# The modulation's 1024-column loads and their bias rows issued by GpSimd instead of SyncE

## The chip, the cores and the metric

The kernel runs on one core of one Trainium2 chip. Five engines work side by side, each on its own instructions in its own fixed order, and wait for one another through semaphores: TensorE (PE) multiplies matrices, VectorE (DVE) and ScalarE (ACT) work on elements, GpSimd (POOL) does small odds and ends, and SyncE (SP) does nothing but issue DMA transfers. The metric is the time of one execution on the device in microseconds (us). A matmul of this kernel mostly multiplies a 128x128 stationary block with 128x512 moving columns.

## What is computed

Two decoder layers over 256 tokens of width 2048. In each layer a conditioning vector is turned into six vectors of length 2048, the modulation, and these shift, scale and gate two sub-layers:

```python
c_act = jax.nn.silu(c)
for l in range(DEPTH):
    mod = c_act @ w_mod[l] + b_mod[l]
    shift1, scale1, gate1, shift2, scale2, gate2 = jnp.split(mod[:, None, :], 6, axis=-1)
    h = rms_norm(x, norm1_gain[l]) * (1.0 + scale1) + shift1
    x = x + gate1 * hybrid_token_mixer(h, ..., w_in[l], ..., w_out[l])
    h = rms_norm(x, norm2_gain[l]) * (1.0 + scale2) + shift2
    x = x + gate2 * swiglu_ffn(h, ffn_w_gate[l], ffn_w_up[l], ffn_w_down[l])
return rms_norm(x, final_norm_gain)
```

The token mixer projects `h` with `w_in`, runs three mixers on parts of the columns (gated linear attention, sliding-window attention, gated delta rule) and projects back with `w_out`. The feed-forward part (FFN) has 5632 hidden columns. All arrays are float32.

## The kernel before

**Weights.** Every projection goes through `stream`: for each block of 128 input rows k (a *job*) SyncE loads 128x1024 weights, 512 KB, into one of three buffers `raw` (L323). ACT rounds them to `wh` (L330), DVE takes the rest `wl = raw - wh` (L331), and PE multiplies with both parts for two blocks of tokens (L358): 12 matmuls for a job. `wh` and `wl` have three buffers each. In some projections the weights are used whole, without L330 and L331.

**Modulation.** `mod @ w_mod` is one vector times a matrix, so it isn't done on PE. `mod_segment` cuts it into segments of 1024 columns with 16 steps each (512 columns for the first two vectors of layer 0, called early). A step loads 512 KB of `w_mod` into one of **two** buffers `mraw` (L220), and DVE multiplies by a column of `c_act` and adds to the accumulator `acc` (L223, a SCALAR_TENSOR_TENSOR, STT below). The first step of a segment clears `acc` on POOL (L212) and loads the bias into its first row (L213). `acc` has two buffers. `finish` sums over the partitions on PE. For the vectors of later use there are 20 such segments with 320 steps; the early ones use buffers `g` and 128 loads of 256 KB.

**What sets the order.** In the program the steps are called from `tick`, so many for each job (`RATE_...`). A scheduler then orders each engine's instructions by the program's priority and by when each could start, and so takes a step ahead of its place in the program where its engine is free and its buffers are. What is on one engine stays in this order on the chip: an instruction whose semaphore is late holds up all that stands behind it. Before the change SyncE issues 1341 rows, with the loads of weights and of the modulation in one row; POOL has 122 rows, among them the small powers for the norms (`rms`, `grs`, `qkrs`, L408), values for the attention's sinks (L891) and the memsets.

## Time and profile before

| | |
|---|---|
| median of 3 runs | 2582.44 us (2582.32 to 2587.12) |
| the profiled execution | 2585.34 us, of which the span 2583.5 us |
| mean granted TensorE clock | 0.986 |
| busy share of the span | PE 94%, DVE 66%, ACT 41%, POOL 2% |
| DMA | 600.79 MB, mean 233 GB/s |
| loads of `w_mod` in steps of 1024 columns | 320 of 512 KB, issued by SPq |
| their work on DVE (L223) | 320 of 1282 ns |

Busy is the time in which an engine had an instruction running; queue and semaphore instructions don't count. SPq is SyncE issuing DMAs. The granted clock is at nine tenths or more in all but one of the profile's 40 slices. A matmul counts as busy while it waits in the pipeline as well, so that how many jobs pass in a stretch says more about PE than its busy share does.

### The profile page before, as it was taken

The page shows a single profiled execution, that of the slowest core. Times are in us where ns is not written, and L with a number is a line of the kernel's source. Part 1 is how long each engine was busy: PE and PEld are TensorE (multiplying, and loading weights), DVE is VectorE, ACT ScalarE, POOL GpSimd, SP SyncE. Part 2 cuts the span into 40 slices and gives each one's busy share as a digit, 9 for nine tenths or more (in the row PEclk, how much of TensorE's full clock was granted, in tenths as well). Part 3 has the DMA queues.
Part 4 walks back from the last instruction along what each step waited for, and adds up shares of the span by engine and source line. Part 5 has one row for each costly group of instructions (what it writes and reads, how often), then busy time and mean ns, then how long its engine had stood idle before and what let it go on. Part 6 is the DMA issues. An engine that isn't in the chain of part 4 may idle for free.

```text
span 2583.5 us, 30803 instructions
## 1 busy us (share of the span) xinstructions
PE 2432.7 (94%) x11164; PEld 1884.1 (73%) x11164; DVE 1714.4 (66%) x2171; ACT 1053.5 (41%) x1548; POOL 58.2 (2%) x117
## 2 busy tenths in 40 slices
PE   4999998889999988999999999999999999999998
PEld 2555785447878767788877878877778878888876
DVE  6767867576675777657578785888664575544555
ACT  2203443124444333344335454564644434344443
POOL 1000000000000000000000000000000000000000
PEclk9999999989999999999999999999999999999999
DMA  9996538777778888868687861675676686666654
GB/s 341 368 322 204 180 114 282 258 231 268 261 259 260 283 268 274 292 193 286 223 277 261 281 192 50 214 232 192 212 256 193 200 286 195 188 191 188 189 184 155
DMA packets 190033, 600.79 MB, mean 233 GB/s; under 512 B 21628, under 2 KB 26268, under 8 KB 189496
## 3 DMA queue, kind: packets, MB, share of 16 engines
q1 hardware_dynamic: 189880, 598.81, 70.7%
q8 instruction: 88, 1.44, 0.2%
q14 instruction: 65, 0.53, 0.1%
HBM read 596.63 MB, written 2.10 MB: 232 GB/s over the span
## 4 chain that ended last, share of the span: by engine, by line
PE 57%; DMA 20%; DVE 10%; issue 8%; ACT 4%; POOL 1%; SPq 1%; DVEq 0%; ACTq 0%; POOLq 0%
PE acc L358 48%; DMA mraw<-in_w_mod 13%; DVE wl L331 4%; DMA raw<-in_w_down 3%; DMA raw<-in_w_in 2%; DVE acc L223 2%; ACT wh L330 1%; PE mm L403 1%; PE ga L895 1%; DMA raw<-in_w_up 1%; PE mm L678 1%; PE mm L685 1%; PE ga L916 1%; DMA raw<-in_w_gate 1%; PE fin L248 1%
## 5 line engine op out<-in xcount | busy, mean ns | idle before, releaser
L358 PE MATMUL acc<-wh,hm 128*128 128x512 f32 (+3 forms) x4872 | 1339.2, 389 | 20.9 <-DVE xs L931 4.7
L330 ACT ACTIVATE wh<-raw 128x1024 fp32r<-128x1024 f32 (+3 forms) x669 | 684.7, 1025 | 985.8 <-PE acc L358 548.9
L331 DVE TENSOR_TENSOR wl<-raw,wh 128x1024 fp32r<-128x1024 f32 (+3 forms) x669 | 785.2, 1179 | 446.6 <-ACT wh L330 444.5
L358 PEld LDWEIGHTS acc<-wh,hm 128*128 128x128 f32 x4872 | 892.0, 189 | 215.8 <-issue 25.5
L358 PE MATMUL acc<-wl,hm 128*128 128x512 f32 (+3 forms) x2484 | 792.3, 394 | 12.2 <-DVE wl L331 9.7
L223 DVE SCALAR_TENSOR_TENSOR acc<-mraw,c_act,acc 128x1024 f32<-128x1024 f32 x320 | 410.3, 1282 | 225.2 <-DMA mraw<-in_w_mod 222.9
L358 PEld LDWEIGHTS acc<-wl,hm 128*128 128x128 f32 x2484 | 458.4, 190 | 124.1 <-DVE wl L331 22.3
L358 PE MATMUL acc<-wh,ahl 128*128 128x512 f32 x560 | 158.4, 397 | 0.0
L358 PEld LDWEIGHTS acc<-wh,ahl 128*128 128x128 f32 x560 | 105.8, 189 | 24.5
L358 PE MATMUL acc<-wl,ahl 128*128 128x512 f32 x280 | 90.8, 398 | 7.2 <-DVE wl L331 7.2
L223 DVE SCALAR_TENSOR_TENSOR g<-g,c_act,g 128x512 f32<-128x512 f32 x128 | 88.7, 747 | 12.6 <-DMA g<-in_w_mod 12.4
L358 PE MATMUL acc<-wh,b 128*128 128x512 f32 (+2 forms) x184 | 74.7, 545 | 2.2 <-ACT b L447 2.1
L358 PE MATMUL acc<-wl,b 128*128 128x512 f32 (+2 forms) x176 | 67.1, 518 | 2.6 <-DVE g L969 2.6
L358 PEld LDWEIGHTS acc<-wl,ahl 128*128 128x128 f32 x280 | 52.2, 189 | 23.1 <-DVE wl L331 11.3
L358 PE MATMUL acc<-raw,b 128*128 128x512 f32 (+2 forms) x176 | 67.6, 524 | 0.0
L358 PEld LDWEIGHTS acc<-wh,b 128*128 128x128 f32 x184 | 35.2, 197 | 30.8 <-issue 23.1
L358 PEld LDWEIGHTS acc<-wl,b 128*128 128x128 f32 x176 | 32.8, 192 | 29.2 <-issue 20.3
L416 ACT ACTIVATE acc<-xs 128x512 f32<-128x512 f32 x32 | 19.0, 595 | 85.7 <-DVE xs L931 85.7
L447 ACT ACTIVATE b<-mm,mod,mod 128x128 f32<-128x128 f32 x24 | 9.2, 461 | 109.7 <-DVE mod L256 92.1
L358 PEld LDWEIGHTS acc<-raw,b 128*128 128x128 f32 x176 | 33.5, 195 | 26.7 <-issue 21.7
L929 DVE TENSOR_TENSOR acc<-acc,gate 128x512 f32<-128x512 f32 x64 | 43.0, 695 | 10.3 <-PE acc L358 10.2
L358 PE MATMUL acc<-raw,hm 128*128 128x512 f32 x88 | 41.7, 598 | 1.4 <-ACT acc L416 1.4
(314 smaller groups left out, 1645.8 us busy)
## 6 DMA issues: line engine op xcount, KB each, us to landing
mraw<-in_w_mod SPq DMA_DIRECT2D x320, 512.0 KB
raw<-in_w_down SPq DMA_DIRECT2D x176, 512.0 KB
raw<-in_w_gate SPq DMA_DIRECT2D x160, 512.0 KB
raw<-in_w_up SPq DMA_DIRECT2D x160, 512.0 KB
raw<-in_w_in SPq DMA_DIRECT2D x72, 512.0 KB
g<-in_w_mod SPq DMA_DIRECT2D x128, 256.0 KB
raw<-in_w_out SPq DMA_DIRECT2D x43, 512.0 KB
raw<-in_w_in SPq DMA_DIRECT2D x32, 264.0 KB
```

Of the source, the lines that this page charges most:

```text
L223: V.scalar_tensor_tensor(acc, raw[:, a], c_act[:, i + a:i + a + 1], acc, ALU.mult, ALU.add)
L248: TE.transpose(ps[:, i * P:(i + 1) * P], acc[:, (j + i) * P:(j + i + 1) * P], ident)
L330: A.activation(wh[:, :width], raw[:, :width], AF.Copy)
L331: V.tensor_tensor(wl[:, :width], raw[:, :width], wh[:, :width].bitcast(F32), ALU.subtract)
L358: TE.matmul(ps[blk, j][:, :segs[j][2]], xa, parts[j][part], start=i == 0 and n == 0, stop=last and n == len(terms) - 1)
L403: TE.transpose(ps[:, j * P:(j + 1) * P], src[:, j * P:(j + 1) * P], ident)
L416: A.activation(scr[0]() if junk is None else junk, xs[:, blk, j * 512:(j + 1) * 512], AF.Square, accum_out=ssq[blk][:, j:j + 1])
L678: TE.matmul(ps[:, s], LT[blk][:, s], Tm[blk][:, s], start=True, stop=True)
L685: TE.matmul(ps[:, s], U[blk][:, s], m1[:, s], start=True, stop=True)
L895: TE.matmul(ps[:, j * nk:(j + 1) * nk], qT[rows, i + j], kT[rows, g, :nk], start=True, stop=True)
L916: TE.matmul(ps[:, j * 64:(j + 1) * 64], pT[:, j * nk + kb * P:j * nk + (kb + 1) * P], kv[kb][:, P + g * 64:P + (g + 1) * 64], start=kb == ...
L929: V.tensor_tensor(ps, ps, need(gate_row, (l, part, j)), ALU.mult)
```

## The change

In `mod_segment` the loads of `mraw` and the bias rows that belong to them are issued with `nc.gpsimd` (`G`) and no longer with `nc.sync` (`SY`). The early steps stay with SyncE, and so do the two buffers `mraw`, the data, the sizes and the arithmetic.

```diff
             if i == 0:
                 st["acc"] = scr[1]() if early else tl(accp, [P, 1024], "acc")
                 G.memset(st["acc"][:, :width], 0.0)
-                SY.dma_start(st["acc"][0:1, :width], b_mod[l:l + 1, c0:c0 + width])
+                (SY if early else G).dma_start(st["acc"][0:1, :width], b_mod[l:l + 1, c0:c0 + width])
             acc = st["acc"][:, :width]
             n = min(rows, KD - i)
             raw = scr[1]() if early else tl(modp, [P, 1024], "mraw")
             if hold:
                 G.tensor_copy(raw[:, 0:1], hold.pop())
             raw = raw[:, :n * width].rearrange("p (a n) -> p a n", a=n)
-            SY.dma_start(raw, w_mod[l, i * P:(i + n) * P, c0:c0 + width]
-                         .rearrange("(a p) n -> p a n", p=P))
+            (SY if early else G).dma_start(raw, w_mod[l, i * P:(i + n) * P, c0:c0 + width]
+                                           .rearrange("(a p) n -> p a n", p=P))
```

SyncE's queue loses 340 rows, 320 loads and 20 bias rows, and POOL's gains them (122 to 462). The scheduler orders all engines anew from there. First the beginning of POOL's queue, before the first norm (`ss` is the sum of squares, `rms` its power, `acc_1231` and `acc_2032` the two halves of the first gate vector of layer 0, `g` an early accumulator):

```order
 L212 MEMSET acc_1231 128x1024
+L220 DMA mraw_1234<-in_w_mod 128x1024
+L213 DMA acc_1231<-in_b_mod 1x16x64
+L220 DMA mraw_1243<-in_w_mod 128x1024
 L212 MEMSET acc_2032 128x1024
+L213 DMA acc_2032<-in_b_mod 1x16x64
+L220 DMA mraw_1246<-in_w_mod 128x1024
 L212 MEMSET g_211 128x512
+L220 DMA mraw_1255<-in_w_mod 128x1024
+L220 DMA mraw_1268<-in_w_mod 128x1024
 L408 ISA
 L408 TENSOR_TENSOR rms_38_179<-ss_37_176,half_100 128x1
```

Five loads of the gate vector now stand ahead of the first norm, at the very start. In SyncE's queue before, they stood behind the weights of nearly the whole first projection (the first was issued at 160.93 us). Twenty of them stand in POOL's queue ahead of the memsets for the last block of that projection.

The same place on DVE, just after the angles' sines are prepared (the rows on `g` are early modulation steps, which the first norm needs):

```order
+L223 SCALAR_TENSOR_TENSOR acc_1231<-mraw_1234,c_act_102,acc_1231 128x1024
+L223 SCALAR_TENSOR_TENSOR acc_1231<-mraw_1243,c_act_102,acc_1231 128x1024
+L223 SCALAR_TENSOR_TENSOR acc_1231<-mraw_1246,c_act_102,acc_1231 128x1024
 L421 TENSOR_REDUCE ss_37_176<-ssp_32_167 128x1
+L223 SCALAR_TENSOR_TENSOR g_205<-g_208,c_act_102,g_205 128x512
 L422 TENSOR_SCALAR ss_37_176<-ss_37_176 128x1
-L223 SCALAR_TENSOR_TENSOR g_205<-g_208,c_act_102,g_205 128x512
+L223 SCALAR_TENSOR_TENSOR acc_1231<-mraw_1255,c_act_102,acc_1231 128x1024
```

Three, then four steps of the gate vector stand ahead of the early steps. Eight have come before the first early sum is complete.

Then DVE in the FFN of layer 0, in the second chunk's gate and up projections (`acc_9745` is a segment of the modulation of layer 1). Before:

```order
L223 SCALAR_TENSOR_TENSOR acc_9745<-mraw_9811,c_act_102,acc_9745 128x1024
L331 TENSOR_TENSOR wl_8272<-raw_8269,wh_8271 128x1024
L331 TENSOR_TENSOR wl_8290<-raw_8287,wh_8289 128x1024
L223 SCALAR_TENSOR_TENSOR acc_9745<-mraw_9850,c_act_102,acc_9745 128x1024
L331 TENSOR_TENSOR wl_8308<-raw_8305,wh_8307 128x1024
L331 TENSOR_TENSOR wl_8329<-raw_8326,wh_8328 128x1024
L223 SCALAR_TENSOR_TENSOR acc_9745<-mraw_9871,c_act_102,acc_9745 128x1024
```

and with the change, on the same engine:

```order
L331 TENSOR_TENSOR wl_8272<-raw_8269,wh_8271 128x1024
L223 SCALAR_TENSOR_TENSOR acc_9745<-mraw_9850,c_act_102,acc_9745 128x1024
L331 TENSOR_TENSOR wl_8290<-raw_8287,wh_8289 128x1024
L223 SCALAR_TENSOR_TENSOR acc_9745<-mraw_9871,c_act_102,acc_9745 128x1024
L331 TENSOR_TENSOR wl_8308<-raw_8305,wh_8307 128x1024
L223 SCALAR_TENSOR_TENSOR acc_9745<-mraw_9892,c_act_102,acc_9745 128x1024
```

Where a step stood for about every one and a half jobs, one now stands for nearly every job. So it is in all ten segments of this kind (eight in the FFN of layer 0, two in that of layer 1): their 16 steps stood among 19 to 24 jobs and stand among 14 to 17. After a segment more jobs follow without a step.

## The prediction

> **What bounds the kernel now.** I read the chain of work that ended last first, then the groups by line, then SyncE's own waits.

> ```profile
> PE 57%; DMA 20%; DVE 10%; issue 8%; ACT 4%; POOL 1%; SPq 1%; DVEq 0%; ACTq 0%; POOLq 0%
> L331 DVE TENSOR_TENSOR wl<-raw,wh 128x1024 fp32r<-128x1024 f32 (+3 forms) x669 | 785.2, 1179 | 446.6 <-ACT wh L330 444.5
> L223 DVE SCALAR_TENSOR_TENSOR acc<-mraw,c_act,acc 128x1024 f32<-128x1024 f32 x320 | 410.3, 1282 | 225.2 <-DMA mraw<-in_w_mod 222.9 <-DMA acc<-in_b_mod 0.2
> SPq L323 <- DVE wl L331: 1343.6, 634, 12.5
> SPq L220 <- DVE acc L223: 221.4, 162, 4.4
> ```

> PE carries the kernel, but a fifth of the chain is DMA, and DVE sat idle for 222.9 us until a modulation load had landed. SyncE waited 221.4 us with such a load at its head until a step had freed one of the two buffers; weights queue behind it meanwhile. The change touches both waits.

> To see what these cost PE I count jobs. L331 runs once for a job, so its count in a stretch is the number of jobs. First come the ten segments in which modulation runs beside the FFN (columns: stretch, its length, DVE busy with L331 and its count, clock, DMA share, GB/s), then two stretches of FFN without any.

> ```profile
> 593.00:663.00 70.00, 29.17 (x24) 1.00 0.87 303
> 686.00:745.00 59.00, 22.98 (x19) 1.00 0.87 297
> 800.00:860.00 60.00, 22.94 (x19) 1.00 0.87 301
> 867.00:937.00 70.00, 26.36 (x22) 0.98 0.84 271
> 945.00:1014.00 69.00, 26.47 (x22) 1.00 0.85 280
> 1022.00:1083.00 61.00, 25.44 (x21) 1.00 0.84 283
> 1169.00:1234.00 65.00, 28.35 (x24) 1.00 0.88 297
> 1287.00:1352.00 65.00, 23.03 (x19) 1.00 0.82 278
> 1846.00:1915.00 69.00, 28.25 (x24) 1.00 0.84 290
> 2067.00:2130.00 63.00, 25.19 (x21) 1.00 0.83 286
> ...
> 2150.00:2310.00 160.00, 70.59 (x58) 1.00 0.61 191
> 2310.00:2470.00 160.00, 69.85 (x57) 1.00 0.62 188
> ```

> Without modulation a job takes 320 us / 115 = 2.78 us, which is PE's own pace. The ten segments have 215 jobs in 651 us; at 2.78 us they would take 598. So modulation beside the FFN costs 53 us now, **5.3 us a segment**, and that is all this change could win there.

> What sets the pace of a segment stands in the chain in order of time (start, length, what):

> ```profile
> 818.49 6.18 DMA mraw<-in_w_mod
> ...
> 825.97 1.23 DVE wl L331
> 827.20 0.02 issue
> 827.22 0.33 SPq L323
> 827.55 0.05 issue
> 827.60 6.86 DMA mraw<-in_w_mod
> ...
> 837.38 5.02 DMA mraw<-in_w_mod
> ```

> This is one buffer going round: a load lands, the step runs (1.28 us by its row above), SyncE still has a weights load ahead that waits for an L331 (1.23), issues it (0.33), and only then the next modulation load. From 827.60 to 837.38 is 9.78 us for one buffer, so 4.9 for a step with two; over the whole segment, 16 steps, about 4.0.

> **The change, part by part.**

> *1. The cycle of a buffer in the FFN.* The weights load ahead goes away: 1.23 + 0.33 and the small gaps, 1.6 us. Left are the landing, (6.18 + 6.86 + 5.02) / 3 = 6.0 us, and the step, 1.28. What POOL adds over SyncE (whose 0.33 or so is in the landing) isn't in this trace, since POOL issues no DMA in it. These are the nearest rows:

> ```profile
> L212 POOL MEMSET g<- 128x512 f32 x8 | 4.4, 552 | 89.3 <-DVE g L223 51.9 <-DMA g<-in_consts 36.2 <-issue 0.8
> L408 POOL TENSOR_TENSOR qkrs<-qkss,half 128x16 f32<-128x16 f32 x2 | 5.8, 2920 | 167.7 <-DVE qkss L596 167.7
> L1032 POOL MEMSET b<- 128x1 f32 x4 | 0.3, 99 | 0.0
> ```

> POOL's cheapest instruction takes 0.1 us and its dearest 2.9; these are the bounds. [...] The cycle is then 6.0 + 1.28 + 0.55 = 7.83 us, or **3.9 us a step** (bounds 3.7 and 5.1; a quicker landing in less traffic, the 5.02 of one piece, gives 3.4).

> What is new is the order. A segment now stands among about 16 jobs on DVE, one step to a job, and DVE can't pass a step whose load is late. PE needs 16 x 2.78 = 44.5 us for these jobs, the steps need 15 x 3.9 = 58.5: 14 us lost. PE has three `wl` buffers and so about one job in hand when a segment starts, 2.8 us of cover that refills where no steps are. 14 - 2.8 = 11.2, less the 5.3 lost already, is 5.9 a segment, **+59 us** for ten. At 3.4 us it is -1.6 a segment (-16), at 5.1 us it is 76.5 - 44.5 - 8.1 = +24 (+240).

> [...]

> *2. The head.* Twenty loads come from 160 us and later into the start. These rows (PE, PEld, DVE, ACT, POOL busy with counts, clock, DMA share, GB/s) show what they meet:

> ```profile
> 20.00:40.00 20.00, 2.23 (x8) 1.43 (x8) 18.13 (x28) 0.00 (x0) 1.05 (x2) 1.00 1.00 361
> 40.00:60.00 20.00, 19.17 (x47) 9.81 (x48) 14.96 (x25) 6.65 (x14) 0.00 (x0) 1.00 1.00 365
> 140.00:160.00 20.00, 20.00 (x66) 11.85 (x65) 12.45 (x22) 0.00 (x0) 0.00 (x0) 1.00 0.99 358
> 180.00:200.00 20.00, 18.93 (x48) 8.24 (x46) 11.14 (x12) 3.42 (x6) 0.00 (x0) 1.00 0.86 281
> 200.00:220.00 20.00, 18.50 (x61) 12.70 (x62) 16.36 (x44) 3.26 (x7) 0.00 (x0) 0.91 0.82 277
> 260.00:280.00 20.00, 15.60 (x78) 11.89 (x79) 17.62 (x37) 8.93 (x26) 0.41 (x1) 0.87 0.65 189
> ```

> ```profile
> 40.83 2.08 PE L358 MATMUL acc<-wh,b 128*128 128x512 f32 x2 [2.09 <-ACT b L447]
> ```

> Until 160 us the DMA engines are full at about 361 GB/s, and PE stands nearly idle for want of the first early sums until its first projection begins at 40.83. By DVE's new order eight gate steps precede these sums, and two further loads are in flight: 10 x 524 KB / 361 GB/s = 14.5 us later for PE's first projection. The other ten loads meet a PE that is full and prefetch that runs ahead; I cost them at nothing, 14.5 us if that cover isn't there. In return DVE is rid of twenty steps between 160 and 280 us. PE sat idle there 1.1 + 1.5 + 4.4 = 7 us, which is the most that can come back. **+8 us** (bounds 0 and +29).

> *3. The output projection of layer 0.* Its weights are used whole; DVE does steps one after the other, for the second norm:

> ```profile
> 401.00:460.00 59.00, 21.78 (x17) 1.00 0.86 288
> 460.00:520.00 60.00, 23.06 (x18) 0.95 0.77 254
> 520.00:559.00 39.00, 15.43 (x13) 0.99 0.84 272
> ```

> 48 steps in 158 us, 3.3 us each, so already at a cycle of 6.6. POOL's 0.55 a cycle would be 48 x 0.275 = 13 us, less what SyncE's order costs there now, which I can't read. Half, **+7 us** (bounds -10 and +68, that is 48 x 2.9 / 2 less nothing).

> *4. POOL's own work.* Twenty powers (L408) now stand behind loads that wait for steps. POOL is 2% busy and a wait is at most a cycle, most of them hidden by PE's other work; **+2 us** (0 to +20).

> *5. Nothing:* the bias rows, 20 of 4 KB, land long before a segment ends; the remaining segments keep their density, and the second half of the last FFN has no modulation.

> Sum: 59 + 8 + 7 + 2 = +76 us. The profiled execution took 2585.3 us, 2.9 above the median of the runs, so on the median's scale 2582.4 + 76 = 2658 us.

> **The rivals.**

> *Weights set free: faster.* SyncE's 221 us at L220 end, weights go out the moment `raw` is free, and two queues side by side shorten the modulation's landing. It decides at the step's pace: with the 17 us of parts 2 to 4 the segments must gain 1.7 each, 15p = 44.5 + 8.1 - 1.7, p = 3.4 us, a cycle of 6.8. For it speaks the landing of 5.02 us in the chain and the 3.3 us a step in the output projection, against it the 6.2 and 6.9 beside FFN weights. At p = 3.0 a segment loses nothing, so -53 from the segments and +8 from the head: 2537 us; at 3.3, -31 and +17: 2568.

> *GpSimd is slow to issue.* With the upper bounds, 240 + 29 + 68 + 20, it would be 2939 us; at 1.5 us an issue, p = 4.4, the segments cost 134 us and the rest some 40: 2756. For it speaks that POOL needs 2.9 us for 128x16 values; against it, the 552 ns memset. [...]

> *No change.* The same bytes and buffers; if the issuer doesn't matter and DVE's denser order is paid back by more jobs without steps, all stays at 2582. [...] Against it stands the order: steps at 4.9 us in the chain above can't keep up with one to every job of 2.78. That the loads don't move can be ruled out: the order on POOL shows them.

> **How the numbers follow.** About 0.2%, 5 us, is what a measurement tells from no change here. Forecast, slower by 20 to 130 us: 0.56. Slow issue, above that: 0.15. Within 0.2%: 0.08. Faster: 0.20, of which the stronger half lies below 2565. The last 0.01 is slower by 5 to 20 us. The likeliest case's own range is 2602 to 2712. For 8 in 10 I leave out half of the faster case and the upper end of the slow one: 2565 to 2780. Faster 0.20, same 0.08, slower 0.72.

> **What would show it.** In the changed profile's ten segments: 14 to 17 jobs beside 16 steps, 3.9 us a step, and DVE's idle time for `mraw` well above 222.9 us; SyncE's wait at L220 gone for all but early loads; the first projection starting near 55 instead of 41 us; and POOL's DMA rows near 0.55 us. I'm wrong if steps take 3.4 us or less, if POOL takes over 1.5 us for a load, or if PE passes its jobs at 2.78 us while DVE waits.

## The result: 4.2% slower, and the profile after

| | before | after |
|---|---|---|
| median (4 runs each, side by side) | 2583.57 us (2582.32 to 2587.12) | 2692.46 us (2687.42 to 2696.51) |
| ratio after / before | | 1.0418, 95% interval 1.0397 to 1.0439 |
| profiled execution, span | 2583.5 us | 2694.6 us |
| mean granted clock | 0.986 | 0.977 |

The change costs 109 us; 76 were forecast. First the chain of work that ended last, by engine and by line:

```profile
PE 46%; DMA 21%; DVE 9%; issue 7%; ACT 1%; POOL 1%; DVEq 0%; POOLq 0%; ACTq 0%; SPq 0%
PE acc L358 41%; DMA mraw<-in_w_mod 18%; DVE acc L223 4%; DVE wl L331 2%; DMA raw<-in_w_down 1%; PE mm L403 1%; DVE acc L929 1%; DMA raw<-in_w_in 1%; DMA raw<-in_w_gate 1%; DVE xs L931 1%; ACT wh L330 1%; PE ga L916 0%; PE ga L895 0%; DMA raw<-in_w_up 0%; PE ga L403 0%
```

PE's share of the chain fell from 57 to 46%, and almost all of the DMA in it is the modulation's loads. Next the steps and the loads that POOL issues (busy, mean ns of one, idle time before them), in the groups by line:

```profile
L223 DVE SCALAR_TENSOR_TENSOR acc<-mraw,c_act,acc 128x1024 f32<-128x1024 f32 x320 | 410.2, 1282 | 259.4 <-DMA mraw<-in_w_mod 250.8
...
L220 POOL DMA_DIRECT2D mraw<-in_w_mod x320 | 170.7, 533 | 1369.4 <-DVE acc L223 840.4
```

And the waits (us in total, times, longest), SyncE's own among them:

```profile
SPq L323 <- DVE wl L331: 1762.2, 641, 23.3
SPq L220 <- DVE g L223: 35.9, 61, 2.8
...
PEld acc L358 <- DVE wl L331: 79.4, 79, 6.0
PE acc L358 <- DVE wl L331: 49.8, 42, 5.8
```

SyncE did lose its 221.4 us at the modulation's loads. But its wait for `raw` to be freed grew from 1343.6 to 1762.2 us: SyncE just comes earlier to a weights load for which there is no buffer. DVE waits only 28 us more for `mraw` than before (250.8 against 222.9), yet PE pays for it: its own waits for `wl` were, before the change,

```profile
PE acc L358 <- DVE wl L331: 16.9, 27, 1.9
```

so they have grown from 16.9 to 49.8 us and the longest of them from 1.9 to 5.8 us.

Third, the ten segments beside the FFN, as before with the count of jobs (stretch, length, DVE busy with L331 and count, clock, DMA share, GB/s):

```profile
633.00:690.00 57.00, 19.26 (x16) 0.97 0.85 299
736.00:780.00 44.00, 16.97 (x14) 1.00 0.94 335
850.00:902.00 52.00, 16.75 (x14) 0.97 0.87 301
902.00:963.00 61.00, 21.43 (x18) 0.94 0.82 286
985.00:1047.00 62.00, 23.77 (x20) 1.00 0.83 288
1072.00:1128.00 56.00, 20.67 (x18) 1.00 0.85 292
1222.00:1282.00 60.00, 22.75 (x19) 0.94 0.85 291
1342.00:1401.00 59.00, 21.87 (x18) 1.00 0.82 288
1938.00:1992.00 54.00, 20.68 (x18) 0.97 0.89 308
2165.00:2224.00 59.00, 21.09 (x18) 0.94 0.83 292
```

(In the second and third of these segments the first step runs far ahead, by 16 and 26 jobs, before by 9 and 19; the stretch holds the other 15.) That is 173 jobs in 564 us; at PE's 2.78 us they would take 481, so 83 us are lost, 8.3 a segment and 3.0 more than before. In the chain in order of time, the cycle of a buffer looks like this:

```profile
861.75 1.30 DVE acc L223
863.04 0.28 issue
863.33 5.02 DMA mraw<-in_w_mod
...
868.44 1.30 DVE acc L223
869.74 0.28 issue
870.02 4.17 DMA mraw<-in_w_mod
...
874.28 1.29 DVE acc L223
```

Step, 0.28 us until POOL takes it up, and 4.2 to 5.0 us of landing with POOL's 0.53 in it: 6.69 and 5.84 us for a buffer, so 3.3 and 2.9 us for a step with two buffers. The forecast had 7.83 and 3.9.

Last, PE's first projection, in the timeline:

```profile
56.38 2.08 PE L358 MATMUL acc<-wh,b 128*128 128x512 f32 x2 [3.16 <-ACT b L447]
```

It begins 15.5 us later than before.

### The profile page after: what moved, and what is told of

The parts are those of the page before. It is cut to its first block, busy times and chain, and to the rows that moved or that the text cites. A ratio compares the mean times of both kernels' runs of the same rounds, so it can differ in the third digit from the quotient of the medians.

```text
span 2694.6 us, 30955 instructions
## 1 busy us (share of the span) xinstructions
PE 2463.3 (91%) x11164; PEld 1895.4 (70%) x11164; DVE 1715.4 (64%) x2171; ACT 1053.9 (39%) x1548; POOL 238.6 (9%) x457
## 2 busy tenths in 40 slices
DMA packets 190633, 600.78 MB, mean 223 GB/s; under 512 B 22248, under 2 KB 26888, under 8 KB 190096
## 3 DMA queue, kind: packets, MB, share of 16 engines
q8 instruction: 87, 1.43, 0.2%
## 4 chain that ended last, share of the span: by engine, by line
PE 46%; DMA 21%; DVE 9%; issue 7%; ACT 1%; POOL 1%; DVEq 0%; POOLq 0%; ACTq 0%; SPq 0%
PE acc L358 41%; DMA mraw<-in_w_mod 18%; DVE acc L223 4%; DVE wl L331 2%; DMA raw<-in_w_down 1%; PE mm L403 1%; DVE acc L929 1%; DMA raw<-in_w_in 1%; DMA raw<-in_w_gate 1%; DVE xs L931 1%; ACT wh L330 1%; PE ga L916 0%; PE ga L895 0%; DMA raw<-in_w_up 0%; PE ga L403 0%
## 5 line engine op out<-in xcount | busy, mean ns | idle before, releaser
L358 PE MATMUL acc<-wh,hm 128*128 128x512 f32 (+3 forms) x4872 | 1355.3, 392 | 25.7 <-ACT wh L330 6.5
L331 DVE TENSOR_TENSOR wl<-raw,wh 128x1024 fp32r<-128x1024 f32 (+3 forms) x669 | 785.0, 1178 | 496.5 <-ACT wh L330 495.9
L330 ACT ACTIVATE wh<-raw 128x1024 fp32r<-128x1024 f32 (+3 forms) x669 | 684.9, 1026 | 1050.3 <-PE acc L358 613.7
L358 PEld LDWEIGHTS acc<-wh,hm 128*128 128x128 f32 x4872 | 901.0, 191 | 224.2 <-issue 19.9
L358 PE MATMUL acc<-wl,hm 128*128 128x512 f32 (+3 forms) x2484 | 804.9, 399 | 56.0 <-DVE wl L331 48.2
L358 PEld LDWEIGHTS acc<-wl,hm 128*128 128x128 f32 x2484 | 461.5, 192 | 179.6 <-DVE wl L331 74.0
L223 DVE SCALAR_TENSOR_TENSOR acc<-mraw,c_act,acc 128x1024 f32<-128x1024 f32 x320 | 410.2, 1282 | 259.4 <-DMA mraw<-in_w_mod 250.8
L220 POOL DMA_DIRECT2D mraw<-in_w_mod x320 | 170.7, 533 | 1369.4 <-DVE acc L223 840.4
L358 PE MATMUL acc<-wh,ahl 128*128 128x512 f32 x560 | 157.6, 395 | 0.1
L358 PEld LDWEIGHTS acc<-wh,ahl 128*128 128x128 f32 x560 | 105.2, 188 | 25.2 <-ACT wh L330 1.0
L223 DVE SCALAR_TENSOR_TENSOR g<-g,c_act,g 128x512 f32<-128x512 f32 x128 | 89.1, 744 | 11.9 <-DMA g<-in_w_mod 11.9
L358 PE MATMUL acc<-wl,ahl 128*128 128x512 f32 x280 | 90.7, 398 | 1.8 <-DVE wl L331 1.6
L358 PE MATMUL acc<-wh,b 128*128 128x512 f32 (+2 forms) x184 | 76.4, 555 | 11.7 <-ACT g L967 7.7
L358 PE MATMUL acc<-wl,b 128*128 128x512 f32 (+2 forms) x176 | 67.3, 523 | 3.8 <-DMA wl<-in_w_in 3.8
L358 PE MATMUL acc<-raw,b 128*128 128x512 f32 (+2 forms) x176 | 66.7, 518 | 1.4 <-DMA raw<-in_w_in 1.4
L358 PEld LDWEIGHTS acc<-wh,b 128*128 128x128 f32 x184 | 35.7, 201 | 42.2 <-issue 25.1
L358 PEld LDWEIGHTS acc<-wl,ahl 128*128 128x128 f32 x280 | 52.1, 188 | 16.9 <-DVE wl L331 5.4
L447 ACT ACTIVATE b<-mm,mod,mod 128x128 f32<-128x128 f32 x24 | 9.1, 458 | 124.8 <-DVE mod L256 107.3
L358 PEld LDWEIGHTS acc<-wl,b 128*128 128x128 f32 x176 | 33.4, 193 | 31.9 <-issue 22.9
L416 ACT ACTIVATE acc<-xs 128x512 f32<-128x512 f32 x32 | 19.1, 596 | 93.5 <-DVE xs L931 93.5
L408 POOL TENSOR_TENSOR rms<-ss,half 128x1 f32<-128x1 f32 x10 | 7.0, 703 | 548.9 <-DVE ss L422 547.7
L358 PEld LDWEIGHTS acc<-raw,b 128*128 128x128 f32 x176 | 32.6, 190 | 27.9 <-issue 21.7
```

The costliest lines, as they stand in the source:

```text
L220: (SY if early else G).dma_start(raw, w_mod[l, i * P:(i + n) * P, c0:c0 + width] .rearrange("(a p) n -> p a n", p=P))
L223: V.scalar_tensor_tensor(acc, raw[:, a], c_act[:, i + a:i + a + 1], acc, ALU.mult, ALU.add)
L330: A.activation(wh[:, :width], raw[:, :width], AF.Copy)
L331: V.tensor_tensor(wl[:, :width], raw[:, :width], wh[:, :width].bitcast(F32), ALU.subtract)
L358: TE.matmul(ps[blk, j][:, :segs[j][2]], xa, parts[j][part], start=i == 0 and n == 0, stop=last and n == len(terms) - 1)
L408: G.tensor_tensor(out, v, half[:, :v.shape[-1]], ALU.pow)
```

## The experiments

**Where the time goes: one part of the loads at a time.** Four kernels give GpSimd only some of the 20 segments and leave the rest to SyncE:

```diff
+        seg[0] += not early
+        pooled = not early and seg[0] in (1, 2)
...
-            (SY if early else G).dma_start(raw, w_mod[l, i * P:(i + n) * P, c0:c0 + width]
+            (G if pooled else SY).dma_start(raw, w_mod[l, i * P:(i + n) * P, c0:c0 + width]
```

The tuple is `(1, 2)` for the head, `(3, 4, 5, 6)` for layer 0's second norm, `(7, 8, 9, 10, 11, 12, 13, 14, 19, 20)` for the FFNs and `(15, 16, 17, 18)` for the start of layer 1. Expected:

> Only the first two segments (GATE1 of layer 0, 32 steps) are issued by GpSimd, all others by SyncE; DVE's order in the head is that of the change, behind it that of before. Order theory (loads on an idle queue are hoisted to the start and meet full DMA engines): the head alone, about +17 us (2600), with the first early sum near 51 us and the FFN segments at 4.0 to 4.7 us a step as before. Path theory (each load that GpSimd issues costs time, whatever its place): 32 of 320 loads, so a tenth of the 109 us, +11. Prediction on record: +8.

> Only segments 3 to 6 (second norm of layer 0, 64 steps, most of them back to back on DVE with no jobs between) are issued by GpSimd. DVE's order hardly changes, so the order theory expects little, 0 to +5 us. The path theory expects the cycle to grow by GpSimd's issue: 48 x 0.27 us and some for the 16 others, +13 to +20 us (2600). In the trace of the full change the stretch from 355 to 597 us grew by 22 us; if this run gives much less, that growth came from steps of the second segment which the hoisting delayed. Prediction on record: +7.

> Only the segments that run beside the FFN (7 to 14, 19 and 20; 160 steps, eight of these segments with 14 to 17 jobs between their steps and not 20 to 24) are issued by GpSimd. Order theory: about 3 us a segment as in the trace of the full change, +23 for layer 0 and +11 for layer 1, so +30 to +36 us (2618). Prediction on record: +59 at 3.9 us a step. A rival, that the segments cost nothing of themselves and are only late from before: below +10.

> Only segments 15 to 18 (the second norm's modulation and GATE1 of layer 1, 64 steps beside its input projection and mixers) are issued by GpSimd. In the full change this stretch (1372 to 1528 us) grew by 28 us, where the prediction had nothing. If that comes from this stretch's own denser order (22 jobs beside a segment instead of 41): +25 to +30 us (2611). If it is an effect of what came late from the FFN: within 5 us of before. If the four parts add up, this run and the three others of this call give 109 us together.

Measured, each against runs of before beside it (us are the ratio's share of 2583):

| by GpSimd | ratio (95% interval) | us | forecast |
|---|---|---|---|
| head, segments 1 and 2 | 1.0078 (1.0052 to 1.0103) | +20 | +8 |
| second norm of layer 0, 3 to 6 | 1.0075 (1.0053 to 1.0096) | +19 | +7 |
| beside the FFNs, 7 to 14, 19, 20 | 1.0173 (1.0130 to 1.0216) | +45 | +59 |
| start of layer 1, 15 to 18 | 1.0105 (1.0081 to 1.0129) | +27 | 0 |
| sum | | +111 | +76 with POOL's 2 |

The parts add up to the whole (109); by their intervals the sum is good to about 15 us. Where in the program each one costs can be read from how much later the same DVE instructions start than before. The first column is a time in before; a figure is the median over all DVE instructions that start there within the next 50 us, from the instruction records. Each kernel has one profiled execution, so the last row need not equal the measured times above.

| us in before | after | head | second norm | FFNs | layer 1 |
|---|---|---|---|---|---|
| 50 | +35 | +35 | +1 | 0 | 0 |
| 300 | +22 | +24 | -3 | -3 | -4 |
| 600 | +40 | +24 | +16 | -5 | -4 |
| 1350 | +63 | +20 | +8 | +18 | -5 |
| 1500 | +91 | +19 | +11 | +19 | +18 |
| 2250 | +107 | +19 | +12 | +40 | +22 |

*Head.* 35 us are lost at once; 11 of them have come back by 300 us and 15 by 1350. In the first 60 us of that run PE has next to nothing to do (PE, PEld, DVE, ACT, POOL busy, clock, DMA share, GB/s by stretch):

```profile
20.00:40.00 20.00, 1.12 (x4) 0.72 (x4) 17.06 (x26) 0.00 (x0) 2.29 (x4) 1.00 1.02 373
40.00:60.00 20.00, 5.85 (x16) 3.40 (x17) 17.09 (x25) 2.79 (x7) 3.18 (x6) 1.00 0.94 321
```

Before, PE had 19.17 us of work in the second of these. The DMA engines are nearly as full as they were (373 and 321 GB/s, before 361 and 365); twenty loads that nobody needs yet, all issued by 97 us, have come in between. What comes back shows in the stretch from 160 to 280 us of before and, 36 us later, in the same stretch of the full change:

```profile
160.00:280.00 120.00, 112.96 (x390) 66.58 (x389) 86.94 (x198) 37.45 (x80) 4.72 (x5) 0.94 0.67 221
```

```profile
196.00:316.00 120.00, 117.88 (x476) 72.55 (x475) 72.66 (x193) 41.05 (x86) 9.92 (x14) 1.00 0.49 148
```

PE's idle time falls from 7.0 to 2.1 us, and its granted clock rises from 0.94 to 1.00, which is worth up to 7 us more of the 120 (an estimate: 0.06 x 120).

*Second norm.* Here DVE's order hardly changes (20, 0, 0 and 1 jobs between the steps of a segment, against 20, 0, 0 and 3), and still it costs 19 us, as the path theory had it. The 32 steps of segments 4 and 5, in the groups by line of their stretch, before and then with GpSimd:

```profile
L223 DVE SCALAR_TENSOR_TENSOR acc<-mraw,c_act,acc 128x1024 f32<-128x1024 f32 x32 | 41.0, 1283 | 30.9 <-DMA mraw<-in_w_mod 30.8
```

```profile
L226 DVE SCALAR_TENSOR_TENSOR acc<-mraw,c_act,acc 128x1024 f32<-128x1024 f32 x32 | 41.0, 1282 | 41.4 <-DMA mraw<-in_w_mod 38.9 <-issue 2.4
```

10.5 us more of idle time for 32 steps is 0.33 a step, 0.66 a cycle, which is a little more than the 0.53 that POOL is busy with a load.

*Start of layer 1.* DVE now takes segment 16 beside 22 jobs, where it was spread over 41, and segment 17 follows at once instead of 100 us later. In the stretch from 1366 to 1570 us the waits are, before and then in this run:

```profile
DVE acc L223 <- DMA mraw<-in_w_mod: 12.9, 14, 1.8
PE acc L358 <- DVE wl L331: 3.0, 5, 1.6
```

```profile
DVE acc L226 <- DMA mraw<-in_w_mod: 23.3, 18, 3.8
PE acc L361 <- DVE wl L334: 12.8, 12, 5.3
```

48 steps lie there and not 32, and PE was busy 176.76 us in place of 189.17 in the 200 us from 1366. So this is the stretch's own denser order, not a lateness handed on.

**Ties on the load.** DVE copies one column of the current job's `wl` into the buffer before its load, so that no load can go out ahead of its place in the program; once with each issuer:

```diff
+            elif tie and not early:
+                V.tensor_copy(raw[:, 0:1], tie[-1])
...
+                tie[:] = [wl[:, 0:1].bitcast(F32)]
```

> All loads on GpSimd as in the change, but each waits for the job of its place in the program: DVE first copies one column of that job's weights into the buffer. So no load is hoisted to the start, and beside the FFN of layer 0 a step comes every 2.5 jobs (7 us), which no cycle of two buffers can miss. More steps are left for layer 1's input projection instead. Order theory: head like before (first early sum near 37 us), no loss in the FFN (below the 53 us that before loses there), some loss at the start of layer 1: between 2560 and 2610. Path theory (GpSimd's loads cost time wherever they stand): 320 loads that cost 109 us now cost about as much, 2660 to 2700.

> The same ties with SyncE as the issuer; DVE's order is nearly the same as in the run with the ties and GpSimd (36 to 38 jobs beside a segment in the FFN in both), so the difference of the two is the path alone. Order theory: 20 us less than that run, since only the back-to-back steps of the second norm see GpSimd's issue (19 us in the run with these alone): 2540 to 2590. Path theory: 60 to 109 us less than that run.

Both were far off: 2911.59 us with GpSimd (ratio 1.1279, 1.1244 to 1.1314) and 2661.08 with SyncE (1.0313, 1.0271 to 1.0354). The timeline of DVE with GpSimd's ties, beside the FFN, shows why:

```profile
922.15 0.15 DVE L220 COPY mraw<-wl 128x1 f32<-128x1 f32 x1
922.23 1.23 DVE L334 TENSOR_TENSOR wl<-raw,wh 128x1024 fp32r<-128x1024 f32 x1
927.34 1.28 DVE L225 SCALAR_TENSOR_TENSOR acc<-mraw,c_act,acc 128x1024 f32<-128x1024 f32 x1 [3.88 <-DMA mraw<-in_w_mod]
928.55 1.22 DVE L334 TENSOR_TENSOR wl<-raw,wh 128x1024 fp32r<-128x1024 f32 x1
```

The tie holds back the load, not only the step, and the scheduler puts the step 1.5 jobs behind the copy (mean of 80 in layer 0's FFN), 4.2 us of PE's work, where copy to step takes 5.9. DVE stands still for the rest and PE runs dry. With SyncE it puts 2.0 jobs between, 5.6 us of work for 5.3 us, and that just holds; there the loss is in layer 1, to which the ties moved steps. By the starts of the same instructions about 114 of the 246 us between the two kernels arise beside that FFN, where half a job of distance differs too, so the pair doesn't tell the path from the order. What it suggests, and the next runs test: what counts is **how many jobs DVE has between the start of a load and its step**.

**Three buffers.** `modp` gets three buffers, and `swa` one less, for both issuers:

```diff
-    modp = ctx.enter_context(tc.tile_pool(name="modp", bufs=2))
+    modp = ctx.enter_context(tc.tile_pool(name="modp", bufs=3))
...
-        pb = bs.enter_context(tc.tile_pool(name=f"swa_{l}", bufs=9, side="right",
+        pb = bs.enter_context(tc.tile_pool(name=f"swa_{l}", bufs=8, side="right",
```

> Three mraw buffers, loads on GpSimd; in return the pool swa has 8 buffers and not 9. The order on DVE is denser still (12 to 14 jobs beside a segment). If the cycle of a buffer (about 7 us) sets the pace, a step now needs 7 / 3 = 2.4 us, and the DMA engines' 361 GB/s (a step and a job in 2.9 us) take over: the segments lose 2 us or less, part of the 109 us comes back, below 2650. If GpSimd's path itself or the density is what costs, the time stays at 2690 or more; the head gets worse in both (three loads early, +20 and more).

> Three mraw buffers with SyncE as the issuer, and the pool swa with 8. If the cycle of a buffer is what binds, the segments lose less than the 5.3 us of before each and the second norm's steps go from 3.4 to about 2.9 us: 2520 to 2560. If weights in SyncE's queue suffer instead from more loads ahead of them: 2580 or more. The difference to the run with three buffers and GpSimd shows how much of the 109 us is the issuer once the cycle doesn't bind.

With GpSimd 2700.51 us (1.0462, 1.0419 to 1.0504), no better than with two; with SyncE 2547.91 (0.9872, 0.9838 to 0.9905), faster than before. The steps' lines, GpSimd first:

```profile
L223 DVE SCALAR_TENSOR_TENSOR acc<-mraw,c_act,acc 128x1024 f32<-128x1024 f32 x320 | 410.0, 1281 | 220.6 <-DMA mraw<-in_w_mod 208.0
```

```profile
L223 DVE SCALAR_TENSOR_TENSOR acc<-mraw,c_act,acc 128x1024 f32<-128x1024 f32 x320 | 410.2, 1282 | 155.7 <-DMA mraw<-in_w_mod 152.8
```

With GpSimd the third buffer is used up by a denser order: most of the segments beside the FFN then have 12 to 14 jobs for 16 steps, and the starts of the steps lie 2.7 to 3.3 us apart; at 12 to 14 jobs of 2.78 us PE runs out all the same. The head is 58 us late at 150 us of the program instead of 36: in the first 175 us 32 loads go out, where the change with two buffers issues 20. With SyncE the queue keeps 19 to 28 jobs beside the segments of layer 0's FFN, and what is gained is gained there and where steps stand back to back. So the cycle of two buffers is not the whole of it: the order has to leave room too. The smaller `swa`, which both runs share, wasn't run by itself.

**Ties on the step.** Now the load is free, and only the step depends on its job, through the column of `c_act`. The rate for layer 0's FFN and one entry of `closed` are changed so that the same eight segments lie there:

```diff
-RATE_FFN = (0.4, 0.25)
+RATE_FFN = (0.5, 0.25)
...
+                if tie and not early:
+                    col = tl(smp, [P, 1], "col", bufs=4)
+                    V.scalar_tensor_tensor(col, tie[-1], 0.0, c_act[:, i + a:i + a + 1],
+                                           ALU.mult, ALU.add)
...
-    closed |= {(l, p) for l in range(1, DEPTH) for p in (SHIFT2, SCALE2)}
```

> SyncE issues. Beside the FFN each step now depends on a weights block of its place in the program (its column of c_act is copied together with 0 times a column of wl), so DVE can't take it early, while its load may go out as soon as a buffer is free; RATE_FFN is 0.5 for layer 0, and the second norm's modulation of layer 1 may run in layer 0's FFN, so that the same eight segments lie there. DVE then has 30 jobs beside each of them (60 in layer 1) and not 20 to 24. If it is the step's place in DVE's order that costs (a step behind too few jobs for its load), the segments lose nothing: 25 to 53 us below before, 2530 to 2555. If a job beside a step costs the same wherever it lies (DMA or DVE share), the time stays within 10 us of before.

> The same with GpSimd as the issuer; beside the FFN DVE's order is the same as in the run with SyncE (30 jobs beside each segment, 60 in layer 1), so there only the path differs. Order theory: the FFN costs no more than with SyncE, and what is left over that run is the head, the second norm of layer 0 and the start of layer 1, 20 + 19 + 27 = 66 us by the runs with one part each. Path theory: the 45 us of the FFN stay too, so 100 us or more above the run with SyncE.

SyncE: 2549.32 us (0.9862, 0.9839 to 0.9884). GpSimd: 2628.72 us (1.0186, 1.0146 to 1.0226), 79 us more. The tied steps, SyncE first, then GpSimd:

```profile
L228 DVE SCALAR_TENSOR_TENSOR acc<-mraw,col,acc 128x1024 f32<-128x1024 f32 x165 | 212.0, 1285 | 14.9 <-DMA mraw<-in_w_mod 9.1
```

```profile
L228 DVE SCALAR_TENSOR_TENSOR acc<-mraw,col,acc 128x1024 f32<-128x1024 f32 x165 | 212.0, 1285 | 25.9 <-DMA mraw<-in_w_mod 19.1
```

The 165 tied steps (of 320) wait for their loads 9.1 us in all with SyncE and 19.1 with GpSimd. The gain of 36 us over before arises beside layer 0's FFN (its end comes 38 us earlier, its start 3); the new rate and `closed` weren't run without the tie, so how much of it is the tie's alone isn't shown. By the starts of the same instructions the run with GpSimd is 46 us behind the one with SyncE at the start of layer 0's FFN, 57 at its end, 66 at 1500 and 76 at the end. Of these 76 us 46 are the head and the second norm, some 14 the start of layer 1 and its mixers, and about 16 arise in the two FFNs (11, and 5 in the second one's first jobs, ahead of its tied steps). The 79 us measured lie nearer to the order theory's 66 than to the 100 or more of the other: with DVE's order the same and 30 jobs beside a segment, the issuer costs 16 us in the FFNs in place of 45.

**Twice GpSimd's time.** A POOL memset of 128x512 goes ahead of each load of the changed kernel:

```diff
+            if not early:
+                G.memset(raw[:, 0:512], 0.0)
             raw = raw[:, :n * width].rearrange("p (a n) -> p a n", a=n)
```

> The change, with a POOL memset of 128x512 (0.55 us) into the buffer ahead of each of its loads: GpSimd's share of the cycle of a buffer doubles. DVE's order beside the FFN stays (15 to 17 jobs a segment); at the start of layer 1 it is nearer to that of before. If the cycle of two buffers sets the pace, a step takes 0.28 us longer where they wait for it: 10 x 15 x 0.28 = 42 us beside the FFN and 48 x 0.28 = 13 in the second norm, less up to 27 at the start of layer 1: 2720 to 2750. If GpSimd's time per load is hidden and only the order costs: 2665 to 2695.

2786.07 us (1.0777, 1.0748 to 1.0805), 93 us above the change and beyond either expectation. The lines of POOL, in the groups by line:

```profile
L220 POOL MEMSET mraw<- 128x512 f32 x320 | 168.8, 528 | 1241.8 <-DVE acc L225 834.6
L222 POOL DMA_DIRECT2D mraw<-in_w_mod x320 | 171.3, 535 | 95.2 <-POOL mraw L220 86.7
```

The memset takes 0.53 us and the load waits another 0.27 for it; the median landing also went from 4.6 to 5.3 us. That is 1.5 us a cycle and not 0.55, and the steps beside the FFN started 0.7 us further apart (half of it) and not 0.28. Why the loads land later isn't known. The direction is plain: where the order leaves no room, a longer cycle shows in the steps' distance and in the time.

**Both cures.** The step's ties and three buffers, with SyncE:

> The steps tied as in the run with ties and SyncE, and three mraw buffers (the pool swa with 8). Alone the ties gave 36 us below before (1.4%) and three buffers 33 (1.3%). Beside the FFN both cure the same loss, so there they don't add; before the FFN (second norm of layer 0) only the third buffer helps: with three buffers the FFN began some 25 us earlier. If so: 55 to 65 us below before, 2515 to 2530. If what the third buffer gains there is given back as GpSimd or PE waits later: 2540 to 2550.

2524.55 us (0.9771, 0.9754 to 0.9788): **2.3% faster than before and 6.2% faster than the change**.

```profile
span 2525.3 us, 30903 instructions
...
PE 69%; DMA 11%; DVE 9%; issue 5%; ACT 4%; POOL 1%; SPq 0%; ACTq 0%; DVEq 0%; POOLq 0%
```

DMA's share of the chain is down from 20% in before to 11.

## Why the prediction was right, and where its terms were off

The sign and the mechanism held: two buffers and a denser order on DVE make steps wait with PE's weights behind them. The total of 109 us lies in the range, 33 above the forecast; the terms were further off than that, in both directions, so that the total comes this near is in part luck.

*1. The cycle beside the FFN: +59 forecast, +45 measured (34 to 56).* 14 to 17 jobs beside 16 steps came as foreseen. The 0.55 us for POOL was an assumption, the time of a memset (L212, 552 ns) put in for that of a load; no run shows 0.55 for a load, and in the change POOL's 320 took 533 ns in the mean. Mis-sized was the landing: 6.0 us was taken from SyncE's loads beside FFN weights, and 0.55 was added to it; the chain shows 4.2 to 5.0 with POOL's part in it. Steps started 3.5 us apart on average over the segments, not 3.9, and half of them 3.2 us or less; that is close to the 3.4 at which the text would have called itself wrong. With 3.5 its own sum is 52.5 - 44.5 - 2.8 - 5.3 = -0.1 us a segment, so no loss at all. Wrong the other way was the cover of 2.8 us: the segments lost 8.3 us each, and 52.5 - 44.5 is 8.0, so the job in hand covered next to nothing. The two errors cancel in part, and that +59 comes near +45 is luck. (In the full change's profile the ten segments show 30 of the 45 us.) That room for the steps takes most of the cost away, with GpSimd too, is what the ties on the step show: 16 us in place of 45.

*2. The head: +8 forecast, +20 measured.* The 14.5 us until PE's first projection were right (15.5). "The other ten loads meet a PE that is full ... I cost them at nothing" was wrong: the lateness goes on growing to 35 us, some 20 more, beyond the 14.5 that the sentence allowed without cover. The step "the most that can come back" was wrong as well: 15 us came back, not 7 at most. It counted PE's idle time and left out the clock, which its own rows show at 0.91 and 0.87; the idle time shrank by 5 us, and the clock at 1.00 in place of 0.94 can account for up to 7 more.

*3. The output projection of layer 0: +7 forecast, +19 measured.* The half price for SyncE's order, which the text said it couldn't read, was wrong; 0.33 us a step over 48 steps is 16, the 13 of the full price and a little. (Its upper bound, 48 x 2.9 / 2, is 70 and not 68.)

*4. POOL's own work: +2.* No run has it apart, and the sum of the four parts, good to about 15 us, can't tell of 2. DVE's waits for POOL's powers sum to 14.4 us before and 13.7 after, which gives no sign of it. Seen was the reverse, a load behind a power: in the run with the second norm alone POOL stood 2.49 us at a `grs` that waited for DVE before it could issue again.

*5. "The remaining segments keep their density": wrong, +27.* This is the step that failed outright. The order would have shown 22 jobs beside segment 16 where there had been 41; the text counted jobs beside the FFN only.

*The rivals.* "Weights set free" fell because SyncE's free time became a wait for `wl` (1343.6 to 1762.2 us). "GpSimd is slow to issue" fell with 533 ns. Nor does DVE's work beside it show in that time: the 158 of POOL's loads that run wholly beside an L331 take 527 ns in the median, and so do the 48 that run while DVE is idle. "No change" fell by 109 us: the bytes are the same (600.79 and 600.78 MB), but the order that one queue had enforced is gone. Over the span two queues moved no more in a second than one: the mean went from 233 to 223 GB/s.

What stays open: how much of the second norm's 0.66 us a cycle is POOL's issue and how much its path, and whether another second queue (ScalarE's) would do the same. Nor was DVE's dense order run with SyncE's loads. At the second norm's 0.33 us a step, GpSimd's path would come to 53 us over the 160 steps beside the FFN (an estimate), as much as the 45 measured there; so within the dense order the path's share and the order's aren't told apart. What the ties on the step show is that most of the cost beside the FFN needs the dense order.

## What to carry to other kernels

A shared queue can also be a brake: here it spaced the loads, and the scheduler, finding them on an idle queue, packed their consumers closer than two buffers could cycle. Before moving a load to another issuer, count on the waiting engine how much work lies between a load and its use, in **every** stage, and compare it with issue + landing + use divided by the buffers (in the chain here 5.84 and 6.69 us by two). To cure late loads, give the consumer its place (not the load) and a buffer more; here that was worth 2.3%, where the other issuer alone cost 4.2%.

## What the hardware showed beside

PE paid for its stalls twice here. It runs the same 11164 matmuls in every one of these kernels, yet its busy time grows with the waits. Before and after:

```profile
PE 2432.7 (94%) x11164; PEld 1884.1 (73%) x11164; DVE 1714.4 (66%) x2171; ACT 1053.5 (41%) x1548; POOL 58.2 (2%) x117
```

```profile
PE 2463.3 (91%) x11164; PEld 1895.4 (70%) x11164; DVE 1715.4 (64%) x2171; ACT 1053.9 (39%) x1548; POOL 238.6 (9%) x457
```

Of the 111 us between the spans 31 are PE's own busy time at a granted clock of 0.977 in place of 0.986; six of the ten segments of the change show 0.94 to 0.97, of before one did, at 0.98. Over the runs it goes from 2411.5 us at 0.991 (ties and three buffers) to 2523.9 at 0.947 (ties on GpSimd's loads).

```profile
867.10:870.50 3.40, 0.59 (x3) 0.17 (x1) 2.06 (x2) 0.78 (x1) 0.48 (x1) 1.00 0.73 265
870.50:873.90 3.40, 2.98 (x7) 2.41 (x8) 2.69 (x3) 0.27 (x1) 0.46 (x2) 0.50 0.75 227
873.90:877.30 3.40, 3.40 (x16) 2.79 (x16) 3.02 (x3) 1.06 (x1) 0.64 (x2) 1.00 0.99 372
```

PE was busy for 0.59 us of the first, got half the clock in the second, where it passed 7 matmuls, and the full clock and 16 matmuls in the third. Cutting all fourteen profiles into stretches of 3.41 us, in step with these changes, gives this count: after a stretch at full clock with PE busy for less than 1.4 us the next was at half in 189 of 189 cases, between 1.4 and 1.8 us in 49 of 133, and after one with 1.8 us or more in 29 of 9,696. So in these profiles every stretch at full clock in which PE stood still for more than 2.0 of its 3.41 us was followed by one at half. PE need not stand still for the whole of it: in the first of the three above it was busy for 0.59 us. PE was busy at half clock for 54 us before and 96 us after; 41 us more at half clock are 21 us of lost work (an estimate), two thirds of the 31. The rest stays open, since busy time isn't a count of the work done: the records of matmuls overlap (from 874.25 us of the change four of L358 stand in 1.08 us, where one lasts 0.39 us in the mean).
